# Within-chunk recurrence by halves at six levels instead of by quarters at three

## The chip, the cores and the metric

The kernel runs on one core of one Trainium2 chip. The metric is device time in microseconds (us) of one execution, taken on that core; the median of three runs is given. Engines are named as the profile names them: PE (matrix multiply, with PEld for its weight loads), DVE (vector), ACT (scalar), POOL (GpSimd) and SP (which issues most DMAs here).

## The reference

The kernel computes one decoder block on 528 tokens (16 learned meta tokens ahead of 512 real ones) with 1024 channels: an input projection into nine parts, a gated linear recurrence with 8 heads of 128 keys and 128 values, a short convolution beside it, a merge with gates, an output projection, and a gated feed-forward net of width 2816 with another short convolution. The part that matters here is the recurrence, whose reference runs over chunks:

```python
def step(S, inp):
    qb, kb, vb, gb = inp
    G = jnp.cumsum(gb, axis=-2)
    o_inter = jnp.einsum('bhtd,bhdv->bhtv', qb * jnp.exp(G), S)
    diff = G[:, :, :, None, :] - G[:, :, None, :, :]
    decay = jnp.exp(jnp.where(causal, diff, -jnp.inf))
    A = jnp.sum(qb[:, :, :, None, :] * kb[:, :, None, :, :] * decay, axis=-1)
    o = o_inter + jnp.einsum('bhts,bhsv->bhtv', A, vb)
    ...
```

So a head needs a score matrix A: for each token t and each earlier token s of the chunk, the sum over 128 keys of q(t) k(s) times the product of the forget gates f of the tokens from s+1 to t. Results are float32.

## The kernel before

**Layout.** Channels lie on the 128 partitions and tokens along the free dimension, so q, k, f of one head are tiles of 128 partitions by 528 tokens (`Qs`, `Ks`, `Fs`, two of each, used by head parity; `V_t` for the values). The kernel treats the 512 real tokens as `NCH` = 4 chunks of 128.

**The large products.** Every weight matrix is split on ACT (`wh`, a cast) and DVE (`wl`, the remainder) into two float32r parts, and each product takes three PE passes (lines 323 to 325 in `product`, 426 to 428 in `raw3`). Most are computed two at a time by `Pair`, a scheme with seven products of half size, whose sums of weights are made on DVE (lines 308, 309, 313).

**The recurrence of one head** is the generator `recur` (line 479). Each `yield` ends a step. Before the levels: V is transposed and POOL prepares the meta tokens' decays. Then come three levels with m = 1, 4, 16 (line 509), each of which joins blocks of m tokens, four at a time, into blocks of 4m. At each level:

- `qv`, 192 columns per chunk, is filled: q of the second, third and fourth quarter (ACT, line 523), q of the third and fourth quarter times one quarter's whole decay (DVE, line 525), q of the fourth times two (line 527). `T` holds the whole decay of each block of m tokens, `F` at the first level.
- Four PE matmuls, one per chunk, take K's 128 tokens as stationary operand and the 192 columns of `qv` as moving operand (line 530). The output is a PSUM tile `psq` of 1024 columns, which is two banks; there is one such buffer, and every other use of the pool (`quarter`) takes it too.
- Q is multiplied by the decays up to its place in the new block (lines 531 to 533), K by the decays after its place (line 541), and the decays of the new blocks are formed (ACT line 537, DVE lines 538 to 540).
- Three masked copies (line 546) put the wanted entries of the scores into A.

After the levels a last join with m = 64 is made by halves (lines 551 to 568): four matmuls of 64 stationary and 64 moving columns (line 554), Q and K multiplied (lines 561, 562), the decays of the 128-token chunks (line 564). Four more steps transpose K, form the states S, apply them and A (lines 597, 598), normalize, and transpose back. That is nine steps.

**Order of the work.** All engines follow the order in which the program is written; the Tile framework adds the waits. The large products call `tick` after every six matmuls of a half-width product. `beat` holds a counter and a period: at each multiple of the period, `tick` runs one step of the oldest waiting `recur`. Between two calls of `merge` there are 62 ticks for head 0 (whose counter begins at -4), 64 for heads 1 to 6, and 42 for head 7. The period is 6, and 4 for head 7. `merge(j)` first runs whatever steps of the head are left, and then uses its output `oS` (lines 745, 746).

Of the kernel before, what the change touches and what calls it, by code (L numbers as in the profile page):

```python
# [7 lines left out]
F32 = mybir.dt.float32  # L8
F32R = mybir.dt.float32r
I32 = mybir.dt.int32  # L10
AF = mybir.ActivationFunctionType
ALU = mybir.AluOpType
PSUM = bass.MemoryType.PSUM

P = 128
D = 1024
KT = D // P
NMETA = 16
SEQ = 512
L = NMETA + SEQ  # L20
# [5 lines left out]
NF = DFF // P  # L26
EPS = 1e-6
NCH = SEQ // P
QW = 192
WARM = 40  # L30
GROUPS = (6, 6, 6, 4)
G0 = EARLY = GROUPS[0]
# [24 lines left out]
def block_kernel(ctx: ExitStack, tc: tile.TileContext, xT, par, wts, pairs, ident, masks, finw, out):  # L57
    nc = tc.nc
    dve, act, pe = nc.vector, nc.scalar, nc.tensor

    const = ctx.enter_context(tc.tile_pool(name="const", bufs=1))
# [2 lines left out]
    whl = ctx.enter_context(tc.tile_pool(name="whl", bufs=4))  # L64
    scan = ExitStack()
    ppair = scan.enter_context(tc.tile_pool(name="ppair", bufs=1, space=PSUM))
    pqk = scan.enter_context(tc.tile_pool(name="pqk", bufs=1, space=PSUM))
    po_pool = scan.enter_context(tc.tile_pool(name="po", bufs=1, space=PSUM))
    pmisc = scan.enter_context(tc.tile_pool(name="pmisc", bufs=1, space=PSUM))

    def scores():
        return pqk.tile([P, 1024], F32, name="psq", tag="psq")

    def quarter():
        return scores()[:, :512].rearrange("p (c n) -> p c n", c=NCH)

    def home(i, dtype=F32, n=528, name="t"):
        return big.tile([P, 528], dtype, name=f"{name}{i}", tag=f"b{i}")[:, :n]
# [1 line left out]
    def pbank(i):  # L80
        return ppair.tile([P, 512], F32, name="pr", tag=f"pr{i}", bufs=1 + (i == 0))
# [48 lines left out]
    beat = [0, 5]  # L130
# [84 lines left out]
    par_t = const.tile([P, NPAR], F32, name="par_t")  # L215
    xt = [home(k, name="xt") for k in range(KT)]
    id_t = const.tile([P, P], F32, name="id_t")
    mk_t = const.tile([P, 3, QW], I32, name="mk_t")
    heads = [fetch(4) for _ in range(2)]

    def load_x(k):
# [190 lines left out]
    rstd = p1.tile([P, L], F32, name="rstd")  # L412
# [38 lines left out]
    with tc.tile_pool(name="rp0", bufs=1) as rp:  # L451
        acc = rp.tile([P, L], F32, name="acc")
        firsts = [(split_unit(raw, 4), [pbank(i) for i in q]) for (raw, _), q in zip(heads, ((1, 2), (0, 0)))]
        for k in range(KT):
            if k % 2 == 0:
                firsts[0][0][2][k // 2]()
            split_scaled(uh[k], ul[k], xt[k], pr("attn", k))
            if k % 2 == 0:
                firsts[1][0][2][k // 2]()
            for (h, lo, _), banks in firsts:  # L460
                for o, at in zip(banks, HALF):
                    raw3(o[:, :HL], h[:, k, :], lo[:, k, :], uh[k][:, at], ul[k][:, at], k == 0, k == KT - 1)
            if k == 5:
                h3rd, l3rd, parts = split_unit(third[0])
                parts[0]()
        for k in range(KT):
            add_square(acc, xt[k], rp, L, k)
        for (_, banks), dst in zip(firsts, (Fs[0], Qs[0])):
            for o, at in zip(banks, HALF):
                act.copy(dst[:, at], o[:, :HL])  # L470
        ahead = [load_unit()]
        both = scores()
        spread_rstd(rstd, acc, lambda i: both[:, 512 * i:512 * i + 512], rp, L)
        raw_unit((h3rd, l3rd), lambda o, at: act.copy(V_t[:, at], o))
    p2 = ph.enter_context(tc.tile_pool(name="ph2", bufs=2))

    M1 = NMETA + 1

    def recur(j, oS):
        b = j % 2  # L480
        K, V, F, Q, A = Ks[b], V_t, Fs[b], Qs[b][:, T0:], As[b]
# [23 lines left out]
        nc.gpsimd.tensor_copy(K0[:, 16:17], K[:, 16:17])  # L505
        T = F[:, M1:]
        Qm = Q[:, NMETA - T0:]
        Km_ = K[:, M1:]
        for lev, m in enumerate((1, 4, 16)):
            nb = P // (4 * m)  # L510
            qv = p2.tile([P, NCH, QW], F32, name="qv", tag="qv")
            q4 = Qm.rearrange("p (c b x) -> p c b x", c=NCH, x=4 * m)
            k4 = Km_.rearrange("p (b s m) -> p b s m", s=4, m=m)
            t4 = T.rearrange("p (c b s) -> p c b s", c=NCH, s=4)
            tf = T.rearrange("p (b s) -> p b s", s=4)
            v1 = qv[:, :, :96].rearrange("p c (b x) -> p c b x", x=3 * m)
            v2 = qv[:, :, 96:160].rearrange("p c (b x) -> p c b x", x=2 * m)
            v3 = qv[:, :, 160:].rearrange("p c (b x) -> p c b x", x=m)

            def tb(i):  # L520
                return t4[:, :, :, i:i + 1].to_broadcast([P, NCH, nb, m])

            act.copy(v1, q4[:, :, :, m:])
            for i in range(2):
                dve.tensor_tensor(v2[:, :, :, i * m:(i + 1) * m], q4[:, :, :, (2 + i) * m:(3 + i) * m],
                                  tb(1 + i), op=ALU.mult)
            dve.tensor_tensor(v3, v2[:, :, :, m:], tb(1), op=ALU.mult)
            ps = scores().rearrange("p (c n) -> p c n", c=NCH)
            for c in range(NCH):
                pe.matmul(ps[:, c, :QW], K[:, M1 + c * P:M1 + (c + 1) * P], qv[:, c, :], start=True, stop=True)  # L530
            dve.tensor_tensor(q4[:, :, :, m:2 * m], q4[:, :, :, m:2 * m], tb(0), op=ALU.mult)
            dve.tensor_tensor(q4[:, :, :, 2 * m:3 * m], v2[:, :, :, :m], tb(0), op=ALU.mult)
            dve.tensor_tensor(q4[:, :, :, 3 * m:], v3, tb(0), op=ALU.mult)
            n4 = SEQ // (4 * m)
            tk = p2.tile([P, n4, 3], F32, name=f"TK{lev}", tag=f"TK{lev}")
            tp = p2.tile([P, n4], F32, name=f"T{lev}", tag=f"T{lev}")
            act.copy(tk[:, :, 2], tf[:, :, 3])
            dve.tensor_tensor(tk[:, :, 1], tf[:, :, 2], tf[:, :, 3], op=ALU.mult)
            dve.tensor_tensor(tk[:, :, 0], tf[:, :, 1], tk[:, :, 1], op=ALU.mult)
            dve.tensor_tensor(tp, tf[:, :, 0], tk[:, :, 0], op=ALU.mult)  # L540
            dve.tensor_tensor(k4[:, :, :3, :], k4[:, :, :3, :], tk.unsqueeze(3).to_broadcast([P, n4, 3, m]),
                              op=ALU.mult)
            a4 = A.rearrange("p c (b x) -> p c b x", x=4 * m)
            for r, lo_, hi_ in ((3, 0, 96), (2, 96, 160), (1, 160, QW)):
                mk = mk_t[:, lev, lo_:hi_].rearrange("p (b x) -> p b x", x=r * m)
                dve.copy_predicated(a4[:, :, :, (4 - r) * m:],  # L546
                                    mk.unsqueeze(1).to_broadcast([P, NCH, nb, r * m]),
                                    ps[:, :, lo_:hi_].rearrange("p c (b x) -> p c b x", x=r * m))
            T = tp
            yield  # L550
        ps = quarter()
        for c in range(NCH):
# [10 lines left out]
        T = p2.tile([P, NCH], F32, name="T128", tag="T128")  # L563
# [44 lines left out]
        ps = quarter()  # L608
# [25 lines left out]
    lo_, hi_ = HALF  # L634
# [150 lines left out]
    s = ring()  # L785
# [23 lines left out]
    for q, sink in enumerate((times(cx0), x_sink, b0_sink, gb0_sink)):  # L809
        unit = ahead.pop()  # L810
        ahead.append(load_unit())
        some(1)
        raw_unit(unit, sink)
        some(1)
        if q == 0:
            beat[:] = [-4, 6]
            begin(0)

    def forget(j):
# [21 lines left out]
    for q, (kind, arg) in enumerate(items):  # L841
        if kind == "m":
            if cur:
                cur.last()
                cur = None
            merge(arg)
            if arg + 1 < KT:
                beat[:] = [0, 6 if arg + 2 < KT else 4]
                begin(arg + 1)
        elif kind == "p":  # L850
            w = pair_weights()
            nxt = Pair(w, arg(), HL, lambda: None)
            if cur:
                cur.last()
            cur = nxt
            cur.middle()
        else:
            unit = ahead.pop() if ahead else load_unit()
            sink = arg() if arg.__name__ == "<lambda>" and arg.__code__.co_argcount == 1 else arg
            half_unit(unit, 0, sink)  # L860
            if cur:
                cur.last()
                cur = None
            some(99)
            half_unit(unit, 1, sink)
# [50 lines left out]
    with tc.tile_pool(name="rp1", bufs=1) as rp:  # L916
        acc = fp2.tile([P, LT], F32, name="acc", tag="fa")
        for k in range(KT):
            ps = mtile(mh, ml, LATE)
# [6 lines left out]
        ps = new_ps()  # L926
# [67 lines left out]
    n = 0  # L994
# [57 lines left out]
    tp = ctx.enter_context(tc.tile_pool(name="tp", bufs=1, side="right"))  # L1052
# [4 lines left out]
    for c in range(NCH):  # L1057
        ps = new_ps()
# [20 lines left out]
def _masks():  # L1079
    import numpy as np  # L1080

    s = np.arange(P)[:, None]
    mk = np.zeros((P, 3, QW), np.int32)
    for lev, m in enumerate((1, 4, 16)):
        at = 0
        for r in (3, 2, 1):
            b, x = np.divmod(np.arange(32 * r), r * m)
            sub = 4 - r + x // m
            mk[:, lev, at:at + 32 * r] = (s // (4 * m) == b) & (s // m % 4 == sub - (4 - r))
            at += 32 * r  # L1090
    return mk


# [50 lines left out]
```

## Time and profile before

| what | value |
|---|---|
| median of 3 runs | 899.25 us (899.13 to 899.52) |
| the profiled execution's own time | 899.76 us |
| its span, first to last instruction | 897.8 us |
| PE busy | 879.7 us, 98% of the span |
| PEld busy | 834.7 us, 93% |
| DVE busy | 735.3 us, 82% |
| ACT busy | 513.4 us, 57% |
| mean granted PE clock | 0.997 of full speed |

The heads' recurrences run from about 37 to 482 us of the span, threaded between the large products. Busy times of PE are those of pipelined instructions, which overlap: an instruction's recorded duration is longer than the distance to the next one, and the distance is what counts for throughput. DVE, ACT and PE each run in their own queue, and a wait in one holds up all that is behind it there.

### The profile page before, as it was taken

What the parts mean: (1) busy time and instruction counts of PE and PEld (TensorE: products, weight loads), DVE (VectorE), ACT (ScalarE), POOL (GpSimd) and SP (SyncE); (2) the same over time, 40 slices, a digit from 0 to 9 for tenths busy, and PEclk for the clock granted to TensorE, in tenths of its full rate; (3) what the DMA queues carried; (4) which work ended last, traced back from release to release, by engine and by line L of the source; (5) the groups of instructions that cost most, each with busy time, mean ns of one, the idle gap of its engine ahead of it and who ended that gap; (6) DMA issues with size and microseconds to landing.
All of it is one profiled execution on the core that took longest, in us unless ns stands there. A gap on an engine that the chain in (4) does not pass through costs nothing.

```text
span 897.8 us, 16494 instructions
## 1 busy us (share of the span) xinstructions
PE 879.7 (98%) x6528; PEld 834.7 (93%) x6528; DVE 735.3 (82%) x1320; ACT 513.4 (57%) x946; POOL 37.1 (4%) x100
## 2 busy tenths in 40 slices
PE   9999999999999999999999999999999999999996
PEld 8998999999999999999999999989999999999984
DVE  7899998989979899899777558985778787777665
ACT  8746657566675575765756346554454545545434
POOL 0211030100101002010000000000000000000000
PEclk9999999999999999999999999999999999999998
DMA  7216344333433443343416321453353443534302
GB/s 257 96 42 203 108 142 134 103 120 116 138 104 118 131 123 118 96 141 101 136 27 199 93 89 60 154 159 117 95 169 113 148 135 114 169 95 125 110 24 93
DMA packets 38813, 108.05 MB, mean 120 GB/s; under 512 B 4305, under 2 KB 5585, under 8 KB 38737
## 3 DMA queue, kind: packets, MB, share of 16 engines
q1 hardware_dynamic: 38448, 106.49, 37.6%
q8 instruction: 51, 0.84, 0.4%
q10 hardware_dynamic: 288, 0.52, 0.2%
q14 instruction: 26, 0.20, 0.1%
HBM read 104.90 MB, written 2.10 MB: 119 GB/s over the span
## 4 chain that ended last, share of the span: by engine, by line
PE 81%; DVE 12%; ACT 3%; issue 2%; DMA 1%; SPq 0%; DVEq 0%; ACTq 0%
PE pr L323 15%; PE pr L325 14%; PE pr L324 14%; PE psm L1009 5%; PE psm L1011 4%; PE psm L1010 4%; PE psm L122 4%; PE psm L120 4%; PE psm L119 4%; PE psq L530 2%; DVE wl L299 2%; PE pr L428 2%; PE pr L426 2%; PE pr L427 2%; DVE A L546 1%
## 5 line engine op out<-in xcount | busy, mean ns | idle before, releaser
L323 PE MATMUL pr<-cm,wh 128*128 128x264 f32 x784 | 227.8, 292 | 1.2 <-DVE za L632 0.7
L324 PE MATMUL pr<-cm,wh 128*128 128x264 f32 x784 | 224.4, 287 | 0.0
L325 PE MATMUL pr<-cm,wl 128*128 128x264 f32 x784 | 223.5, 286 | 0.0
L323 PEld LDWEIGHTS pr<-cm,wh 128*128 128x128 f32 x784 | 147.3, 188 | 4.0 <-issue 1.6
L325 PEld LDWEIGHTS pr<-cm,wl 128*128 128x128 f32 x784 | 147.7, 189 | 0.2
L324 PEld LDWEIGHTS pr<-cm,wh 128*128 128x128 f32 x784 | 147.5, 188 | 0.0
L298 ACT CAST wh<-wt 128x1024 fp32r<-128x1024 f32 x88 | 92.6, 1053 | 84.2 <-PE pr L324 44.3
L299 DVE TENSOR_TENSOR wl<-wt,wh 128x1024 fp32r<-128x1024 f32 x88 | 106.9, 1216 | 27.5 <-ACT wh L298 27.5
L100 DVE TENSOR_TENSOR wl<-wr,wh 128x1024 fp32r<-128x1024 f32 (+1 forms) x64 | 71.8, 1126 | 39.1 <-ACT wh L99 37.9
L99 ACT CAST wh<-wr 128x1024 fp32r<-128x1024 f32 (+1 forms) x64 | 61.6, 967 | 67.1 <-PE psm L120 30.2
L331 ACT COPY c<-pr 128x264 f32<-128x264 f32 (+1 forms) x132 | 49.5, 375 | 41.0 <-PE pr L325 36.4
L323 PE MATMUL pr<-cf,wh 128*128 128x258 f32 x256 | 72.5, 283 | 0.0
L324 PE MATMUL pr<-cf,wh 128*128 128x258 f32 x256 | 72.1, 282 | 0.0
L325 PE MATMUL pr<-cf,wl 128*128 128x258 f32 x256 | 71.9, 281 | 0.0
L299 DVE TENSOR_TENSOR wl<-wr,wh 128x1024 fp32r<-128x1024 f32 x44 | 53.8, 1222 | 13.1 <-ACT wh L298 13.0
L298 ACT CAST wh<-wr 128x1024 fp32r<-128x1024 f32 x44 | 46.1, 1048 | 20.6 <-PE pr L324 19.4
L323 PE MATMUL pr<-cb,wh 128*128 128x258 f32 x192 | 54.7, 285 | 0.3 <-ACT xr L970 0.3
L308 DVE TENSOR_TENSOR wt<-wt 128x1024 f32<-128x1024 f32 x44 | 53.7, 1220 | 1.4 <-DMA wt<-in_pairs 1.1
L324 PE MATMUL pr<-cb,wh 128*128 128x258 f32 x192 | 54.7, 285 | 0.0
L325 PE MATMUL pr<-cb,wl 128*128 128x258 f32 x192 | 54.4, 283 | 0.0
L324 PEld LDWEIGHTS pr<-cf,wh 128*128 128x128 f32 x256 | 48.6, 190 | 0.8
L323 PEld LDWEIGHTS pr<-cf,wh 128*128 128x128 f32 x256 | 48.1, 188 | 0.7
(291 smaller groups left out, 2282.7 us busy)
## 6 DMA issues: line engine op xcount, KB each, us to landing
wr<-in_wts SPq DMA_DIRECT2D x56, 512.0 KB, 3.7
wr<-in_pairs SPq DMA_DIRECT2D x44, 512.0 KB, 4.1
wt<-in_pairs SPq DMA_DIRECT2D x44, 512.0 KB, 4.0
wt<-in_pairs SPq DMA_DIRECT2D x88, 256.0 KB, 4.7
xt<-in_xT SPq DMA_DIRECT2D x8, 264.0 KB, 4.8
xr<-in_xT SPq DMA_DIRECT2D x8, 264.0 KB, 3.5
out<-xr SPq DMA_DIRECT2D x8, 256.0 KB, 2.2
wr<-in_wts SPq DMA_DIRECT2D x8, 128.0 KB, 4.5
```

Of the source, the lines that this page charges most:

```text
L99: act.copy(h[:, i:i + n, :], raw[:, i:i + n, :])
L100: dve.tensor_tensor(lo[:, i:i + n, :], raw[:, i:i + n, :], h[:, i:i + n, :].bitcast(F32), op=ALU.subtract)
L119: pe.matmul(o, wh, rh[:, a:b], start=first, stop=False)
L120: pe.matmul(o, wh, rl[:, a:b], start=False, stop=False)
L298: act.copy(h, src)
L299: dve.tensor_tensor(lo, src, h.bitcast(F32), op=ALU.subtract)
L308: dve.tensor_tensor(t[:, 1:3, :], t[:, 1:3, :], t[:, 3:, :].to_broadcast([P, 2, 512]), op=ALU.add)
L323: pe.matmul(ps, h[:, j], ch, start=start and j == 0, stop=False, skip_group_check=True)
L324: pe.matmul(ps, h[:, j], cl, start=False, stop=False, skip_group_check=True)
L325: pe.matmul(ps, lo[:, j], ch, start=False, stop=j == 3, skip_group_check=True)
L331: act.copy(c, r)
L1009: pe.matmul(o, gh, wh, start=first, stop=False)
```

## The change

The three levels by quarters become six levels by halves, with m = 1, 2, 4, 8, 16, 32 (`LEVELS`). A level joins blocks of m tokens, two at a time. The only scores it needs are those of each second half's q against the first half's k, 64 columns per chunk, and these columns are read where they lie in Q, with a stride of 2m, so that `qv` and its ACT copy and DVE multiplies are gone. Q's second halves are then multiplied by the first half's decay, K's first halves by the second half's, the decays of neighbours are multiplied together, and one masked copy of 64 columns per chunk takes the scores into A. The last join with m = 64 and all that follows it are as before.

The PSUM pool `pqk` now has two buffers of one bank each instead of one of two banks. The masks become six of 64 columns instead of three of 192. A head has twelve steps instead of nine, and the periods go from 6 to 5, and from 4 to 3 for head 7.

```diff
-QW = 192
+LEVELS = (1, 2, 4, 8, 16, 32)
...
-    pqk = scan.enter_context(tc.tile_pool(name="pqk", bufs=1, space=PSUM))
+    pqk = scan.enter_context(tc.tile_pool(name="pqk", bufs=2, space=PSUM))
...
-    def scores():
-        return pqk.tile([P, 1024], F32, name="psq", tag="psq")
-
     def quarter():
-        return scores()[:, :512].rearrange("p (c n) -> p c n", c=NCH)
+        return pqk.tile([P, NCH, P], F32, name="psq", tag="psq")
...
-    mk_t = const.tile([P, 3, QW], I32, name="mk_t")
+    mk_t = const.tile([P, len(LEVELS), 64], I32, name="mk_t")
...
-        both = scores()
-        spread_rstd(rstd, acc, lambda i: both[:, 512 * i:512 * i + 512], rp, L)
+        banks = [pqk.tile([P, 512], F32, name="psq", tag="psq") for _ in range(2)]
+        spread_rstd(rstd, acc, lambda i: banks[i], rp, L)
...
-        for lev, m in enumerate((1, 4, 16)):
-            nb = P // (4 * m)
-            qv = p2.tile([P, NCH, QW], F32, name="qv", tag="qv")
...
-            act.copy(v1, q4[:, :, :, m:])
-            for i in range(2):
-                dve.tensor_tensor(v2[:, :, :, i * m:(i + 1) * m], q4[:, :, :, (2 + i) * m:(3 + i) * m],
-                                  tb(1 + i), op=ALU.mult)
-            dve.tensor_tensor(v3, v2[:, :, :, m:], tb(1), op=ALU.mult)
-            ps = scores().rearrange("p (c n) -> p c n", c=NCH)
+        for lev, m in enumerate(LEVELS):
+            nb = P // (2 * m)
+            n2 = SEQ // (2 * m)
+            q2 = Qm.rearrange("p (n h m) -> p n h m", h=2, m=m)
+            k2 = Km_.rearrange("p (n h m) -> p n h m", h=2, m=m)
+            t2 = T.rearrange("p (n h) -> p n h", h=2)
+            ps = quarter()
             for c in range(NCH):
-                pe.matmul(ps[:, c, :QW], K[:, M1 + c * P:M1 + (c + 1) * P], qv[:, c, :], start=True, stop=True)
-            dve.tensor_tensor(q4[:, :, :, m:2 * m], q4[:, :, :, m:2 * m], tb(0), op=ALU.mult)
-            dve.tensor_tensor(q4[:, :, :, 2 * m:3 * m], v2[:, :, :, :m], tb(0), op=ALU.mult)
-            dve.tensor_tensor(q4[:, :, :, 3 * m:], v3, tb(0), op=ALU.mult)
...
-            act.copy(tk[:, :, 2], tf[:, :, 3])
-            dve.tensor_tensor(tk[:, :, 1], tf[:, :, 2], tf[:, :, 3], op=ALU.mult)
-            dve.tensor_tensor(tk[:, :, 0], tf[:, :, 1], tk[:, :, 1], op=ALU.mult)
-            dve.tensor_tensor(tp, tf[:, :, 0], tk[:, :, 0], op=ALU.mult)
-            dve.tensor_tensor(k4[:, :, :3, :], k4[:, :, :3, :], tk.unsqueeze(3).to_broadcast([P, n4, 3, m]),
-                              op=ALU.mult)
...
-            for r, lo_, hi_ in ((3, 0, 96), (2, 96, 160), (1, 160, QW)):
-                mk = mk_t[:, lev, lo_:hi_].rearrange("p (b x) -> p b x", x=r * m)
-                dve.copy_predicated(a4[:, :, :, (4 - r) * m:],
...
-            T = tp
+                pe.matmul(ps[:, c, :64].rearrange("p (b m) -> p b m", m=m), K[:, M1 + c * P:M1 + (c + 1) * P],
+                          q2[:, c * nb:(c + 1) * nb, 1, :], start=True, stop=True)
+            dve.tensor_tensor(q2[:, :, 1, :], q2[:, :, 1, :], t2[:, :, 0:1].to_broadcast([P, n2, m]), op=ALU.mult)
+            dve.tensor_tensor(k2[:, :, 0, :], k2[:, :, 0, :], t2[:, :, 1:2].to_broadcast([P, n2, m]), op=ALU.mult)
+            Tn = p2.tile([P, n2], F32, name=f"T{lev}", tag=f"T{lev}", bufs=1)
+            dve.tensor_tensor(Tn, t2[:, :, 0], t2[:, :, 1], op=ALU.mult)
+            T = Tn
+            dve.copy_predicated(A.rearrange("p c (b h m) -> p c b h m", h=2, m=m)[:, :, :, 1, :],
+                                mk_t[:, lev, :].rearrange("p (b m) -> p b m", m=m).unsqueeze(1)
+                                .to_broadcast([P, NCH, nb, m]),
+                                ps[:, :, :64].rearrange("p c (b m) -> p c b m", m=m))
             yield
...
-            beat[:] = [-4, 6]
+            beat[:] = [-4, 5]
...
-                beat[:] = [0, 6 if arg + 2 < KT else 4]
+                beat[:] = [0, 5 if arg + 2 < KT else 3]
...
-    mk = np.zeros((P, 3, QW), np.int32)
...
+    mk = np.zeros((P, len(LEVELS), 64), np.int32)
+    for lev, m in enumerate(LEVELS):
+        mk[:, lev] = (s // (2 * m) == np.arange(64) // m) & (s // m % 2 == 0)
     return mk
```

More of the change, by code (lines that the diff above doesn't have):

```diff
@@ L508, in recur @@
         Km_ = K[:, M1:]
-        for lev, m in enumerate((1, 4, 16)):
-            nb = P // (4 * m)
-            qv = p2.tile([P, NCH, QW], F32, name="qv", tag="qv")
[L512 to L523, printed above, removed]
-            for i in range(2):
-                dve.tensor_tensor(v2[:, :, :, i * m:(i + 1) * m], q4[:, :, :, (2 + i) * m:(3 + i) * m],
-                                  tb(1 + i), op=ALU.mult)
-            dve.tensor_tensor(v3, v2[:, :, :, m:], tb(1), op=ALU.mult)
-            ps = scores().rearrange("p (c n) -> p c n", c=NCH)
-            for c in range(NCH):
-                pe.matmul(ps[:, c, :QW], K[:, M1 + c * P:M1 + (c + 1) * P], qv[:, c, :], start=True, stop=True)
-            dve.tensor_tensor(q4[:, :, :, m:2 * m], q4[:, :, :, m:2 * m], tb(0), op=ALU.mult)
-            dve.tensor_tensor(q4[:, :, :, 2 * m:3 * m], v2[:, :, :, :m], tb(0), op=ALU.mult)
-            dve.tensor_tensor(q4[:, :, :, 3 * m:], v3, tb(0), op=ALU.mult)
[L534 to L538, printed above, removed]
-            dve.tensor_tensor(tk[:, :, 0], tf[:, :, 1], tk[:, :, 1], op=ALU.mult)
-            dve.tensor_tensor(tp, tf[:, :, 0], tk[:, :, 0], op=ALU.mult)
-            dve.tensor_tensor(k4[:, :, :3, :], k4[:, :, :3, :], tk.unsqueeze(3).to_broadcast([P, n4, 3, m]),
-                              op=ALU.mult)
-            a4 = A.rearrange("p c (b x) -> p c b x", x=4 * m)
-            for r, lo_, hi_ in ((3, 0, 96), (2, 96, 160), (1, 160, QW)):
-                mk = mk_t[:, lev, lo_:hi_].rearrange("p (b x) -> p b x", x=r * m)
-                dve.copy_predicated(a4[:, :, :, (4 - r) * m:],
-                                    mk.unsqueeze(1).to_broadcast([P, NCH, nb, r * m]),
-                                    ps[:, :, lo_:hi_].rearrange("p c (b x) -> p c b x", x=r * m))
-            T = tp
@@ L1082, in _masks @@
     s = np.arange(P)[:, None]
-    mk = np.zeros((P, 3, QW), np.int32)
[L1084 to L1090, printed above, removed]
+    mk = np.zeros((P, len(LEVELS), 64), np.int32)
+    for lev, m in enumerate(LEVELS):
+        mk[:, lev] = (s // (2 * m) == np.arange(64) // m) & (s // m % 2 == 0)
     return mk
```

## The prediction, made before the changed kernel was run

> **What bounds the kernel now.** I read the page first, then what PE waits for, then PE's timeline around the matmuls that the change touches, then the rows of the DVE and ACT instructions that go. The page's busy times, and its chain of waits by engine:
>
> ```profile
> PE 879.7 (98%) x6528; PEld 834.7 (93%) x6528; DVE 735.3 (82%) x1320; ACT 513.4 (57%) x946; POOL 37.1 (4%) x100
> PE 81%; DVE 12%; ACT 3%; issue 2%; DMA 1%; SPq 0%; DVEq 0%; ACTq 0%
> ```
>
> PE is busy 98% of the time and holds 81% of the chain. The chain's 12% on DVE looks like a second bound, but it is not 12% that could be won: where PE waits 0.5 us for DVE, the chain changes to DVE and follows it back through everything that it did back to back. What a faster DVE can win is what PE really waits. Those waits of PE that lie in the recurrences' stretch are these (total us, times, longest):
>
> ```profile
> PE psq L554 <- DVE A L546: 1.3, 2, 1.0
> PE pr L428 <- DVE wl L100: 1.0, 2, 0.5
> PE psq L579 <- ACT Km L576: 0.7, 1, 0.7
> PE pr L323 <- DVE za L632: 0.7, 1, 0.7
> PE psq L530 <- DVE qv L525: 0.6, 1, 0.6
> PE psm L119 <- DVE z L726: 0.5, 1, 0.5
> PE pm L612 <- DVE om L606: 0.5, 1, 0.5
> PE pr L323 <- ACT c L331: 0.5, 1, 0.5
> PE po L597 <- ACT S L583: 0.4, 1, 0.4
> PE psq L530 <- DVE qv L527: 0.2, 1, 0.2
> ```
>
> They sum to 6.4 us in 12 waits. A wait costs a little more than its row says, since PE counts as busy until its pipeline has drained. The longest one, in the timeline (start, length, instruction, count, idle time before):
>
> ```profile
> 407.69 0.28 PE L325 MATMUL pr<-cm,wl 128*128 128x264 f32 x1
> 409.01 0.65 PE L554 MATMUL psq<-Q,K 128*64 128x64 f32 x8 [1.04 <-DVE A L546]
> ```
>
> Without the wait L554 would have started one product distance (0.12 us, below) after 407.69; it started 1.20 us later than that, of which the row shows 1.04. So a wait costs 0.16 us beyond its row, and the 12 cost 6.4 + 12 x 0.16 = 8.3 us. That is all that lies within reach of a lighter DVE and ACT; the rest of this stretch is PE going from matmul to matmul. So the question is how much PE time the change adds or takes.
>
> **PE: the price of one pass.** A float32 matmul is issued as two passes, each with its own load of the stationary operand: line 530 runs 12 times for each of 8 heads, and the trace has 192 of it (lengths of single passes, which overlap: minimum, median, maximum in ns).
>
> ```profile
> L530 PE MATMUL psq<-qv,K x192: 323/326/402, 48.1 to 457.2; 128*128 128x192 f32 x192
> L197 PE MATMUL psq<-onesD,acc x10: 242/250/250, 21.2 to 22.2; 128*128 128x1 f32 x10
> L554 PE MATMUL psq<-Q,K x64: 222/222/271, 67.9 to 462.3; 128*64 128x64 f32 x64
> ```
>
> The distance from one pass to the next comes out of the timeline's merged rows: the length of the row less that of one pass, over the count less one.
>
> ```profile
> 396.35 0.28 PE L325 MATMUL pr<-cm,wl 128*128 128x264 f32 x1
> 396.47 1.46 PE L530 MATMUL psq<-qv,K 128*128 128x192 f32 x8
> ...
> 397.89 0.28 PE L427 MATMUL pr<-cm,wh 128*128 128x264 f32 x1
> 398.01 0.28 PE L428 MATMUL pr<-cm,wl 128*128 128x264 f32 x1
> ...
> 21.23 1.25 PE L197 MATMUL psq<-onesD,acc 128*128 128x1 f32 x10 [0.25 <-DVE acc L176]
> ...
> 425.16 0.28 PE L325 MATMUL pr<-cm,wl 128*128 128x264 f32 x1
> 425.28 0.38 PE L597 MATMUL po<-S,Q 128*128 128x128 f32 x2
> ...
> 427.18 0.28 PE L324 MATMUL pr<-cm,wh 128*128 128x264 f32 x1
> ```
>
> - 192 moving columns, 128 stationary: (1.46 - 0.326) / 7 = 162 ns. The whole insert agrees: from 396.35 to 397.89 are 1.54 us, less two product distances of 0.12 (397.89 to 398.01) is 1.30, or 8 x 162 ns. Such an insert costs nothing at its edges.
> - 128 moving, 128 stationary: from 425.16 to 427.18, less 0.24, are 1.78 us for the 16 passes of lines 597 and 598: 111 ns.
> - 1 moving, 128 stationary: (1.25 - 0.250) / 9 = 111 ns.
> - 64 moving, 64 stationary (line 554, row above): (0.65 - 0.222) / 7 = 61 ns.
>
> From 192 to 128 moving columns the distance falls, and from 128 to 1 it no longer does. So 111 ns is a floor that the 128 stationary float32 columns set, with the moving columns passing beside their load; line 554 goes lower with half as many. **The new matmuls have 64 moving columns but still 128 stationary ones** (a whole chunk of K), so I give each pass 111 ns, as in the rows on either side, 1 and 128.
>
> The Trainium skill has two rules that part here. "TensorE: Matmul & The Clock Gate", section "Back-to-back issue gap", lists about 60 cycles (25 ns) for a matmul of up to 64 columns; by that the 384 new passes are an estimated 9.6 us against 31.1 now, 21.5 us gained. Its section "LDWEIGHTS (loading the stationary operand)" has the load scale with the stationary columns alone, 107 ns for 128 of them; by that they are an estimated 41.1 us, 10.0 lost. The trace sides with the second: 111 ns at one moving column, 61 at half the stationary ones.
>
> Per head before: 24 passes x 162 = 3.89 us. After: 6 levels x 4 chunks x 2 = 48 passes x 111 = 5.33 us. **PE gets 1.44 us more work a head, 11.5 us over 8 heads**, and it is the bound all through this stretch: + 11.5.
>
> **DVE and ACT: what goes.** What the levels hold now, and the nearest rows to what they will hold (the row with the sum is line 546 in one stretch per head):
>
> ```profile
> L525 DVE TENSOR_TENSOR qv<-Q,T x32: 261/282/490, 55.5 to 451.2; 128x128 f32<-128x128 f32 x32
> L525 DVE TENSOR_TENSOR qv<-Q,F x16: 378/397/416, 46.3 to 400.6; 128x128 f32<-128x128 f32 x16
> L538 DVE TENSOR_TENSOR TK<-T x16: 164/190/210, 57.7 to 414.1; 128x32 f32<-128x32 f32 x8, 128x8 f32<-128x8 f32 x8
> L538 DVE TENSOR_TENSOR TK<-F x8: 389/438/471, 48.4 to 402.3; 128x128 f32<-128x128 f32 x8
> L541 DVE TENSOR_TENSOR K<-K,TK x24: 545/552/608, 50.0 to 458.2; 128x384 f32<-128x384 f32 x24
> sum 246.00, DVE 38.95; mean DVE 4.87
> L546 DVE COPY_PREDICATED A<-mk_t,psq 128x256 f32<-128x256 int32 x24 | 12.9, 538 | 0.0
> L561 DVE TENSOR_TENSOR Q<-Q,T x8: 407/414/425, 68.8 to 462.5; 128x256 f32<-128x256 f32 x8
> L523 ACT COPY qv<-Q x24: 497/514/518, 37.3 to 447.7; 128x384 f32<-128x384 f32 x24
> ACT qv L523 <- PE psq L530: 12.9, 15, 1.0
> ACT TK L537 <- DVE T L540: 10.5, 12, 1.4
> ```
>
> Now, per head: 18 multiplies of 128 elements (lines 525, 527, 531 to 533), 12 at 0.28 and the first level's 6 at 0.40, are 5.8 us; 9 of lines 538 to 540, 6 at 0.19 and 3 at about 0.4, are 2.3; line 541 is 1.7; the masked copies 4.9. That is 14.7 us. After: six times Q and K (0.41 each) and one masked copy of 256 elements (0.54) are 8.2 us, and six products of decays, from 256 elements down to 8, at 0.19 to 0.44 are about 1.5: 9.7 us. DVE loses 5 us a head; ACT loses its copies (0.51 us three times a head) and the 23 us in which its queue stood behind them (the last two rows).
>
> None of this is on PE's path except through the 8.3 us. Of the waits, L530's two and L554's two (2.1 us, 2.7 with the drain) belong to what the change takes away: L530 waits for `qv`, made in its own step, while the new matmuls read Q and K as the step before left them; and L554 waits for the masked copies to give back the one `psq`, of which there are now two. These count as won. Four rows (L428, L323 after `za`, L579, L597: 2.8 us in 5 waits, 3.6 with the drain) come from queues that are late, and the trace has the first head as the stretch without slack on DVE:
>
> ```profile
> 30.00:97.00 67.00, 63.99 (x501) 61.19 (x500) 65.49 (x139) 41.44 (x84) 10.95 (x20) 1.00 0.36 116
> ```
>
> (The length of the stretch, then PE, PEld and DVE busy: DVE 65.5 of 67 us.) I count half of the 3.6 as won, since the splits and sums in that queue stay. The last three (L119, L612, L323 after `c`) stand near the ends of heads, and I count none. Together 4.5 us won, between 0 (waits only move) and 8.3.
>
> **What is added beside PE's passes.** The multiplies of Q and K must wait until the level's matmuls have read them, and the masked copy until they have written. Behind them on DVE stand the `wl` splits and the sums of the pairs, for which PE's later products wait. This happens six times a head instead of three. Two levels are 5 ticks apart, 30 products of 0.12 us and the level's own 0.9: 4.5 us, for 0.8 us of DVE work (Q and K) that the next level needs. For head 7 it is 3 ticks, 2.2 + 0.9 = 3.1 us. Head 0 reaches 55 as its last multiple of 5, so `merge` runs its twelfth step; DVE's line 745 then waits for the transposes and their copy, some 1 us at most, while PE goes on with the next pair's first product, which needs none of it. No row shows what an insert pays whose operands DVE has only just finished; the bounds are nothing (L530's edges) and one drain of 0.16 for each of 24 inserts more, 3.8. I take 1.0 for all of this, nearer the row of the same kind. The masks' transfer shrinks by a third and nothing early waits for it, and `spread_rstd` uses two buffers where it used two halves of one: nothing.
>
> **Sum.** Against the profiled execution's own 899.76 us: + 11.5 - 4.5 + 1.0 = + 8.0, so 907.8. That execution is 0.5 above the median of the runs shown; for the median, 899.25 + 8.0 = **907.2 us**.
>
> **Rivals.**
>
> 1. *The load does not set the distance* (this ends on the other side). If the load of K's columns hides, and the 111 ns at one moving column has another cause, the new passes go at line 554's 61 ns: 384 x 61 = 23.4 us against 31.1, 7.7 gained, and with the 3.5 (4.5 less 1.0) 899.25 - 7.7 - 3.5 = 888.0. It decides from the distance at which 384 passes take 31.1 + 3.5: below 90 ns the change gains. For it speaks that no row has 64 moving on 128 stationary; against it, that the rows on either side both say 111. The issue-gap rule above is its strongest form. Chance 0.10, half of it between.
> 2. *All waits go.* 899.25 + 11.5 - 8.3 = 902.5. For it, DVE's 65.5 of 67 us in the first stretch; against it, that the last three waits stand far from the levels. Still slower, since 11.5 exceeds all that PE waits. Chance 0.08.
> 3. *Head 7's closer steps wait.* DVE does runs of three long operations there:
>
> ```profile
> 445.27 1.22 DVE L299 TENSOR_TENSOR wl<-wt,wh 128x1024 fp32r<-128x1024 f32 x1
> 446.41 1.22 DVE L308 TENSOR_TENSOR wt<-wt 128x1024 f32<-128x1024 f32 x1
> 447.54 1.22 DVE L299 TENSOR_TENSOR wl<-wt,wh 128x1024 fp32r<-128x1024 f32 x1
> ```
>
>    If one such run (3.6 us) falls between two levels, the next comes 3.6 + 0.8 - 3.1 = 1.3 us late; once for each of head 7's three pairs, 3.9 us in place of the 1.0: 910.1. It decides from 2.3 us of other work between two levels. Against it, PE waited for `qv` at only two of the 24 levels before, though `qv` is made in the level's own step on the same queue. Chance 0.14.
> 4. *Strided reads.* At m = 1 Q is read with a stride of two elements. DVE's rows (397 against 282 ns at the first level) show that strides can cost. PE has room: at 61 ns the columns may pass 1.8 times slower inside 111. At three times, 183 ns, the 128 passes of two levels would cost 72 ns more each, 9.2 us: 916.4. Chance 0.03.
>
> The forecast itself has 0.65.
>
> **Numbers.** The range runs from the case in which all waits go, 902.5, to 912.0, which holds rival 3 and the edges at their most (907.2 - 1.0 + 3.8 = 910.0) with 2 us for waits that aren't won. It leaves out rival 1 and rival 4. A measurement of this kernel tells about 0.2%, 1.8 us, from no change. Slower by more than that is everything but rival 1, 0.90; rival 1 gives 0.05 faster and 0.05 within.
>
> **What would show it.** Right: 384 passes in the levels' line, in merged rows of 8 that last about 0.25 + 7 x 0.111 = 1.03 us; few waits of PE on the levels' tiles; DVE some 40 us less busy; 1.4 us more PE work a head. Wrong: such rows near 0.68 us, waits of PE for Q, K or `psq` in head 7, or a time under 901.

## The result, and the profile after

| | before | changed kernel |
|---|---|---|
| median | 899.19 us (898.96 to 899.52, 4 runs) | 910.18 us (909.49 to 911.37, 4 runs) |
| ratio | | 1.0123, 95% interval 1.0106 to 1.0141 |
| profiled execution: own time, span | 899.76, 897.8 us | 911.37, 909.6 us |

The changed kernel is slower, 11.0 us by the medians and 11.6 by the two profiled executions. The page's busy times and chain of waits after:

```profile
PE 892.8 (98%) x6720; PEld 848.4 (93%) x6720; DVE 715.4 (79%) x1200; ACT 498.9 (55%) x898; POOL 31.4 (3%) x100
PE 94%; DVE 2%; ACT 1%; DMA 1%; issue 0%; SPq 0%; ACTq 0%; DVEq 0%
```

PE is busy 13.1 us longer and holds 94% of the chain, where it held 81%; DVE's 12% of the chain are down to 2%, and that bought no time. One insert of a level in PE's timeline, with products before and after it:

```profile
227.41 0.28 PE L322 MATMUL pr<-cm,wl 128*128 128x264 f32 x1
227.53 1.00 PE L514 MATMUL psq<-Q,K 128*128 128x64 f32 x8
228.34 0.37 PE L320 MATMUL pr<-cm,wh 128*128 128x264 f32 x1
228.55 0.28 PE L321 MATMUL pr<-cm,wh 128*128 128x264 f32 x1
```

From 227.41 to 228.55 are 1.14 us; less two product distances of 0.12 the insert takes 0.90, or 112 ns for each of its 8 passes. The 33 other inserts that stand whole between two products, with no wait beside them, take 0.89 or 0.90, but for one of 1.06. An insert took 1.30 before, but there were half as many. The very first level of a head, whose columns are read with a stride of two elements, takes the same (222.85 to 223.99 in head 2):

```profile
222.85 0.29 PE L322 MATMUL pr<-cm,wl 128*128 128x264 f32 x1
222.98 1.00 PE L514 MATMUL psq<-Q,K 128*128 128x64 f32 x8
223.79 0.37 PE L423 MATMUL pr<-cm,wh 128*128 128x264 f32 x1
223.99 0.28 PE L424 MATMUL pr<-cm,wh 128*128 128x264 f32 x1
```

What PE waits for in the recurrences' stretch (total us, times, longest), and one wait of DVE:

```profile
PE pr L425 <- DVE wl L97: 3.0, 1, 3.0
PE pr L320 <- ACT c L328: 1.3, 1, 1.3
PE psm L116 <- DVE z L701: 0.5, 1, 0.5
PE pm L587 <- DVE om L581: 0.2, 1, 0.2
...
DVE Q L516 <- PE psq L514: 17.7, 32, 1.3
```

Together they are 5.0 us in 4 waits, where the kernel before had 6.4 in 12. The waits on the levels' tiles are gone: no row of PE names line 514 or 529 (the old 530 and 554). DVE's new wait at each level, 17.7 us in all, reaches PE nowhere as a row of its own. But there is one wait of 3.0 us, longer than any before, and a second of 1.3. The first, on PE and on DVE's queue:

```profile
66.66 0.59 PE L425 MATMUL pr<-cm,wl 128*128 128x264 f32 x1 [2.98 <-DVE wl L97]
67.04 0.42 PE L423 MATMUL pr<-cm,wh 128*128 128x264 f32 x1
67.26 0.42 PE L424 MATMUL pr<-cm,wh 128*128 128x264 f32 x1
...
72.32 0.32 PE L425 MATMUL pr<-cm,wl 128*128 128x264 f32 x1
72.48 0.29 PE L423 MATMUL pr<-cm,wh 128*128 128x264 f32 x1
72.61 0.29 PE L424 MATMUL pr<-cm,wh 128*128 128x264 f32 x1
```

```profile
59.16 0.43 DVE L516 TENSOR_TENSOR Q<-Q,T 128x256 f32<-128x256 f32 x1 [0.43 <-PE psq L514]
59.50 0.70 DVE L365 TENSOR_TENSOR cm<-ct,cm 128x528 fp32r<-128x528 f32 x1
60.12 0.70 DVE L391 TENSOR_TENSOR ct<-hn 128x528 f32<-128x528 f32 x1
60.74 0.70 DVE L379 TENSOR_TENSOR ct<-hn 128x528 f32<-128x528 f32 x1
61.36 0.42 DVE L517 TENSOR_TENSOR K<-K,T 128x256 f32<-128x256 f32 x1
...
65.35 1.26 DVE L97 TENSOR_TENSOR wl<-wr,wh 128x1024 fp32r<-128x1024 f32 x1
```

Two things are to be seen. The weight split that PE waits for (line 97) stands in DVE's queue behind a run of sums for later products (lines 365 to 391). And the queue isn't in the written order: lines 516, 517, 519 and 521 are written one after another, but three operations of other work stand between 516 and 517. So my sentence that all engines follow the order in which the program is written was wrong: the queues get an order of their own, and a change in one place can move instructions in another (wide_move, below, changes only the levels' matmuls and their masked copy, and there this split starts at 57.61 instead of 65.35). What sets the order was not looked into.

The second thing is what the wait did to PE's clock. Products came 0.22 us apart from 67.04 on, and 0.12 apart again from 72.5. The windows' row for that stretch (length, DVE busy, granted clock, then DMA):

```profile
65.00:75.00 10.00, 7.54 (x15) 0.66 0.69 239
```

In the kernel before, the granted clock is 1.00 throughout the same stretch. From 66.66 to 72.32 some 26 products took 0.10 us more each, about 2.6 us. So this one wait cost some 3.1 us of standing still and 2.6 of half speed. In windows of 1 us the clock falls at about 65.6, 1.9 us into the idle time, and is back at 72.4, after 6.8 us at half. The same wait of 3.0 us stands in two of the runs below: in half_load the clock fell 1.2 us into it and stayed at half for 6.8 us, in after_phase at its end, and for 3.4 us. So the cost in clock is not the same each time, and the 2.6 us are those of this execution, the longest of the changed kernel's four. "TensorE: Matmul & The Clock Gate" in the Trainium skill has PE return to half rate after an idle window of about 3.4 us that runs freely (section "What's actually happening"); the trace agrees on the half rate, and 3.4 and 6.8 us at half would be one and two such windows, but here 3.0 us idle were enough, and the clock had fallen before they were over.

### The profile page after: what moved, and what is told of

Its sections match the earlier page's. It is cut to its first block, busy times and chain, and to the rows that moved or that the text cites. A ratio compares the mean times of both kernels' runs of the same rounds, so it can differ in the third digit from the quotient of the medians.

```text
span 909.6 us, 16754 instructions
## 1 busy us (share of the span) xinstructions
PE 892.8 (98%) x6720; PEld 848.4 (93%) x6720; DVE 715.4 (79%) x1200; ACT 498.9 (55%) x898; POOL 31.4 (3%) x100
## 4 chain that ended last, share of the span: by engine, by line
PE 94%; DVE 2%; ACT 1%; DMA 1%; issue 0%; SPq 0%; ACTq 0%; DVEq 0%
PE pr L320 17%; PE pr L321 16%; PE pr L322 16%; PE psm L984 4%; PE psm L986 4%; PE psq L514 4%; PE psm L985 4%; PE psm L119 4%; PE psm L116 4%; PE psm L117 4%; PE pr L425 3%; PE pr L423 3%; PE pr L424 3%; PE psq L556 1%; PE po L573 1%; PE po L572 1%
## 5 line engine op out<-in xcount | busy, mean ns | idle before, releaser
L320 PE MATMUL pr<-cf,wh 128*128 128x258 f32 x256 | 72.5, 283 | 0.0
```

What stands on the lines that cost most here:

```text
L320: pe.matmul(ps, h[:, j], ch, start=start and j == 0, stop=False, skip_group_check=True)
```

## The experiments

Theory L was that the load of the stationary operand sets the price of a pass, so that twice the loads are the loss. Its rival M was that the price goes by moving columns, and the loss came from the steps. (A price that each pass has whatever it loads is a third reading; only half_load tells it from L.) On the 1.3 and 3.0 us waits, theory W put them on the closer steps, and V on the order of the queues.

**Twice the loads alone (cut_two).** The kernel before, with each matmul in two:

```diff
-pe.matmul(ps[:, c, :QW], K[:, M1 + c * P:M1 + (c + 1) * P], qv[:, c, :], start=True, stop=True)
+for u, w in ((0, 128), (128, QW)):
+    pe.matmul(ps[:, c, u:w], K[:, M1 + c * P:M1 + (c + 1) * P], qv[:, c, u:w], start=True, stop=True)
```

> The kernel before, by quarters, with each matmul of 192 moving columns cut into one of 128 and one of 64 on the same stationary chunk of K: as many loads as the change makes (48 passes a head instead of 24), the same columns, the same DVE and ACT work, steps and periods. Theory L (the load of 128 stationary columns sets the price of a pass, 111 ns): 384 passes x 111 ns = 42.6 us against 31.1, so 899.2 + 11.5 = 910.7 us, within 2 us for waits that move. Rival M (the price goes by moving columns, and the loss came from the steps by halves): 2304 columns a head as before, so 899.2 us.

Measured: 909.88 us against 899.37, ratio 1.0105 (1.0086 to 1.0125). One level of it:

```profile
281.46 0.28 PE L428 MATMUL pr<-cm,wl 128*128 128x264 f32 x1
281.58 1.89 PE L531 MATMUL psq<-qv,K 128*128 128x128 f32 x16
283.28 0.37 PE L426 MATMUL pr<-cm,wh 128*128 128x264 f32 x1
283.49 0.28 PE L427 MATMUL pr<-cm,wh 128*128 128x264 f32 x1
```

From 281.46 to 283.49, less 0.24, are 1.79 us for 16 passes, 112 ns each, whether they move 128 columns or 64. Over 24 inserts, 1.79 for 1.30 is 11.8 us. Twice the loads, with no column more and nothing else in the program changed, cost 10.5 us, about what the whole change cost; some of PE's waits moved as well (4.4 us in this stretch for 6.4, with a new one of 2.1 us for ACT's line 606). M falls.

**Twice the columns alone (wide_move).** The changed kernel, with all of a chunk's Q moving:

```diff
-pe.matmul(ps[:, c, :64].rearrange("p (b m) -> p b m", m=m), K[:, M1 + c * P:M1 + (c + 1) * P],
-          q2[:, c * nb:(c + 1) * nb, 1, :], start=True, stop=True)
+pe.matmul(ps[:, c, :], K[:, M1 + c * P:M1 + (c + 1) * P], Qm[:, c * P:(c + 1) * P], start=True, stop=True)
...
-                    ps[:, :, :64].rearrange("p c (b m) -> p c b m", m=m))
+                    ps.rearrange("p c (b h m) -> p c b h m", h=2, m=m)[:, :, :, 1, :])
```

> The changed kernel, with all 128 columns of a chunk of Q as moving operand, read without stride, instead of the 64 that are needed; the masked copy takes the same entries. Theory L: the columns pass beside the load, so 112 ns a pass as before, 910.2 us within 1.5. Rival M: at 0.8 ns a column (the difference of the rows for 192 and 128) 64 columns more are 51 ns a pass, 19.6 us, 929.8 us. If the stride in Q had cost something, this would be faster than 910.2.

Measured: 905.81 us, ratio to the kernel before 1.0062 (1.0043 to 1.0080), so 4.4 us *faster* than the changed kernel and not 19.6 slower. One level:

```profile
222.47 0.28 PE L322 MATMUL pr<-cm,wl 128*128 128x264 f32 x1
222.59 1.05 PE L514 MATMUL psq<-Q,K 128*128 128x128 f32 x8
223.40 0.37 PE L320 MATMUL pr<-cm,wh 128*128 128x264 f32 x1
223.61 0.28 PE L321 MATMUL pr<-cm,wh 128*128 128x264 f32 x1
```

From 222.47 to 223.61, less 0.24: 0.90 us, what 64 columns took. Twice the columns are free beside the load. The 4.4 us can therefore not come from the stride, which my expectation had offered as the reading of a faster time; the passes' price is the same. They fit head 0's 5.7, less two waits that are new here (0.8 us for line 580, 0.4 for line 517): this kernel has no wait of PE for line 97 at all, since its queues came out in another order, and its clock is 1.00 there. The same split in DVE's queue:

```profile
57.61 1.22 DVE L97 TENSOR_TENSOR wl<-wr,wh 128x1024 fp32r<-128x1024 f32 x1
```

That was the first sign for V.

**Half the load (half_load).** The changed kernel, with 64 stationary columns:

```diff
-pe.matmul(ps[:, c, :64].rearrange("p (b m) -> p b m", m=m), K[:, M1 + c * P:M1 + (c + 1) * P],
+pe.matmul(ps[:64, c, :64].rearrange("p (b m) -> p b m", m=m), K[:, M1 + c * P:M1 + c * P + 64],
           q2[:, c * nb:(c + 1) * nb, 1, :], start=True, stop=True)
```

(The masked copy takes 64 partitions accordingly.)

> The changed kernel, with only the first 64 tokens of each chunk as stationary operand of a level's matmul, so that scores of the other 64 against later tokens are left out; as many matmuls, moving columns and DVE instructions. Theory L: a pass costs what line 554 showed for 64 stationary columns, 61 ns, so 384 x (112 - 61) = 19.6 us less than the changed kernel, 910.2 - 19.6 = 890.6 us, up to 3 more where DVE can no longer keep up. Rival M (moving columns or a fixed cost of each pass): no change, 910.2 us.

Measured: 905.64 us, ratio 1.0059 (1.0036 to 1.0082): 4.5 us less than the changed kernel, where L had said 19.6 and M nothing. The trace shows why L was short:

```profile
224.70 0.28 PE L322 MATMUL pr<-cm,wl 128*128 128x264 f32 x1
224.91 0.68 PE L514 MATMUL psq<-Q,K 128*64 128x64 f32 x8
225.52 0.39 PE L320 MATMUL pr<-cm,wh 128*128 128x264 f32 x1
225.75 0.28 PE L321 MATMUL pr<-cm,wh 128*128 128x264 f32 x1
```

Within the insert the passes do come 65 ns apart, (0.68 - 0.222) / 7, as line 554 had shown. But from 224.70 to 225.75, less 0.24, are 0.81 us, and 8 x 65 ns are 0.52: an insert of narrower stationary operands pays 0.29 us at its edges. Against 0.90 that is 0.09 saved for each of 48 inserts, 4.3 us, which is what was measured; 38 inserts of this run lie between 0.80 and 0.84, and head 0's wait and half clock are in it as in the changed kernel. So L stands for the distance between passes, and a price that each pass has whatever it loads falls. My expectation failed by edges that I had not counted. They could have been seen in the kernel before, at line 554:

```profile
461.61 0.28 PE L324 MATMUL pr<-cm,wh 128*128 128x264 f32 x1
461.82 0.68 PE L554 MATMUL psq<-Q,K 128*64 128x64 f32 x8
462.43 0.39 PE L325 MATMUL pr<-cm,wl 128*128 128x264 f32 x1
462.66 0.28 PE L323 MATMUL pr<-cm,wh 128*128 128x264 f32 x1
```

From 461.61 to 462.66, less 0.24, are 0.81 us here too: 101 ns a pass with the edges, where within the row they are 61 to 65 ns apart. What makes them was not tried.

**The periods alone (periods).** The kernel before, with 5 and 3 for 6 and 4:

```diff
-beat[:] = [-4, 6]
+beat[:] = [-4, 5]
...
-beat[:] = [0, 6 if arg + 2 < KT else 4]
+beat[:] = [0, 5 if arg + 2 < KT else 3]
```

> The kernel before with the periods of the change, 5 and 3 instead of 6 and 4, and nothing else. The changed kernel has two new long waits of PE, 3.0 us in head 0 and 1.3 us at the end of head 7. Theory W (the closer steps make them): they come here too, and with L530's own waits the time is 902 to 904 us. Rival V (they come from the order in which DVE and ACT stand in their queues, which is planned anew for each kernel): no such pair here, 899.2 us within 1.5.

Measured: 898.47 us, ratio 0.9986 (0.9976 to 0.9997). Closer steps cost the kernel by quarters nothing, and its longest wait in the levels' stretch is 0.6 us:

```profile
PE psq L530 <- DVE A L546: 0.7, 2, 0.6
```

W falls for these levels; on the levels by halves the periods were not changed alone.

**Head 0's split, earlier (after_early).** If the order of DVE's queue is the cause, moving one split up is the cure:

```diff
 unit = ahead.pop() if ahead else load_unit()
+if q < 2:
+    ahead.append(load_unit())
```

> The changed kernel, with the second and third weight units of head 0's row of single units loaded and split one unit earlier in the program, nothing else. In the changed kernel's DVE queue that split (line 97, at 65.35 us) stands behind ten operations of the combinations and PE waits 3.0 us for it. Theory V (the planned order of DVE's queue in head 0 ate the gain that I had counted): the wait goes, 910.2 - 3 to 4.5 = 905.7 to 907.2 us. Rival D (DVE has too much to do there in any order): the wait moves to a later unit and the time stays within 1 us of 910.2.

Measured: 907.10 us (906.77 to 907.60), ratio 1.0089 (1.0075 to 1.0102), 3.1 us less than the changed kernel. In the written order, too, the split had stood behind those sums, and the edit puts it ahead of them. It now starts at 56.94, and the longest waits of PE in the recurrences' stretch are:

```profile
PE pr L320 <- ACT c L328: 1.3, 1, 1.3
...
PE pm L587 <- DVE om L581: 0.9, 1, 0.9
PE pr L322 <- DVE wl L296: 0.6, 1, 0.6
```

The 3.0 us wait and the half clock behind it are gone. Two waits of 0.9 (0.2 before) and 0.6 came in their place, so that 4.2 or so of the 5.7 us of wait and clock should come back. The two profiled executions are 4.5 apart (911.37 and 906.91), the medians 3.1; the changed kernel's profiled execution is its longest, and of its others no trace is kept. V holds for head 0, as far as the place in the queue goes: what the edit moved is the split, and the wait went with it.

**Head 7, one tick earlier (after_phase).** For the other wait, 1.3 us for ACT's line 328:

```diff
-beat[:] = [0, 5 if arg + 2 < KT else 3]
+beat[:] = [0, 5] if arg + 2 < KT else [1, 3]
```

> The changed kernel, with head 7's counter beginning at 1 instead of 0, so that each of its steps comes one tick earlier. In the changed kernel PE waits 1.3 us at 489 us for ACT line 328, which stands behind the square root of head 7's eleventh step. If the place of that step beside the pair's products makes the wait, it shrinks to the 0.5 us that it had before: 909.2 us; if the wait comes from ACT's work there in any order, 910.2 us as it was.

Measured: 910.14 us (909.11 to 911.62). The wait is what the first theory said:

```profile
PE pr L320 <- ACT c L328: 0.5, 1, 0.5
```

What stands ahead of line 328 in the changed kernel is shown by ACT's queue:

```profile
489.06 1.28 ACT L183 ACT_TABLE_LOAD   x1
490.36 0.21 ACT L183 ACTIVATE ryo<-rvo 128x5 f32<-128x5 f32 x1
490.47 0.36 ACT L328 COPY c<-pr 128x264 f32<-128x264 f32 x1
```

It is less the square root itself, 0.21 us, than the load of its table, 1.28 us. In after_phase that load comes at 485.56, behind a copy of line 328 and 2.5 us ahead of the next. The time did not follow within what its runs can show: 0.04 us less, where 1.0 was expected, with runs spread over 2.5 us. That the tick's place made the wait is shown by the trace; that it is worth 1 us is not.

**The kernel by quarters, with both (periods_early).** The two edits above that had not hurt, on the kernel before:

> The kernel before, with the periods 5 and 3 and with the second and third weight units of head 0 split one unit earlier. If what is left of PE's waits in head 0 (L428 for line 100, 0.9 us with two drains of 0.16) goes: 898.5 - 1.2 = 897.3 us; if DVE is full there in any order: 898.5 us. Either way under the 899.2 of the kernel before.

Measured: 896.55 us (895.75 to 897.77, 8 runs), ratio 0.9971 (0.9961 to 0.9981), the fastest of all here, 2.6 us under the kernel before and 13.6 under the changed one. The longest that is left in the levels' stretch:

```profile
PE psq L530 <- DVE A L546: 1.0, 2, 0.6
PE pr L323 <- ACT c L331: 0.6, 1, 0.6
PE pr L428 <- DVE wl L100: 0.5, 1, 0.5
```

It gained 1.9 over the periods alone (1.7 when each is held against the kernel before that was measured beside it), where I had said 1.2, though L428's wait only went from 0.9 to 0.5; which of the small waits made the rest, I can't tell from these rows.

## Why the prediction was right, and where not

I had said 907.2 us, 902.5 to 912.0, slower; it is 910.18.

- *The bound.* Right. PE's share of the chain rose from 81% to 94%. The chain's share on DVE fell from 12% to 2% and nothing was won by it: as the prediction argued, it had been the path's detour over short waits.
- *The price of a pass, 111 ns, + 11.5 us.* Right: 112 in the trace, for 64 columns as for 128. 48 inserts of 0.90 us for 24 of 1.30 are + 12.0, and cut_two, with the loads alone, cost 10.5 in its medians.
- *DVE and ACT.* Line by line right (Q and K at 0.42, a head's levels near 9.7 us), but DVE's busy time fell by 20 us and not by 40. The recorded lengths of the levels' lines did fall by 41 us (119 to 78). Such a sum overstates what goes: DVE's operations overlap, and in the rows above an operation of 0.70 us is followed by the next after 0.62.
- *Waits won, - 4.5.* This is the step that failed. Its first part, 2.7 us for the waits on `qv` and on the one `psq`, came true: both are gone. Its second, "half of the 3.6" of the queues that are late in the first head, did not. I had read those waits as DVE having too much to do, and given it less; what counted was where an instruction stands in its queue, and the order came out anew. In its place came one wait of 3.0 us, and a half clock that no part of the prediction had, some 5.7 us together, where the five waits had been 3.6. In all, the four waits left in this stretch are 5.0 us, 5.6 with the drains and 8.2 with the clock, against 8.3 in the kernel before: nothing was won, which is the lower bound that I had named (waits only move). With the passes' 12.0 that gives the 11.6 by which the two profiled executions differ, within half a microsecond. after_early shows the cause: with the split moved up, the wait and the half clock go. That its 907.1 is the forecast to 0.1 us is partly luck, since the waits left there (1.3, 0.9, 0.6, 0.5) are not the ones that I had counted as left.
- *What is added, + 1.0.* The edges of the inserts were nothing, as at L530. Head 0's twelfth step made no wait that I could find. The wait at the end of head 7 grew from 0.5 to 1.3; after_phase shows that it hangs on the tick at which the square root's table load falls, not on the number of steps.
- *Rivals.* The first is out (cut_two, wide_move). Its price was misread besides: line 554's 61 ns leave out the edges, and with them its 8 passes take 0.81 us, so 48 such inserts would have been 38.9 us against 31.1, 7.8 lost and not 7.7 gained. The second would have needed all waits gone; they did not go. The third named head 7, and PE waits for nothing at the levels there; periods shows the closer steps harmless on the levels by quarters. The fourth is out: the first level's insert takes 0.90 us like the others.

## What to carry to other kernels

Count a small float32 matmul by its stationary load first: with 128 stationary columns anything up to 128 moving columns cost the same 112 ns here, so halving the moving columns and doubling the matmuls is a loss on a bound PE, and widening the moving operand up to there is free. A lighter engine off the path pays only where PE waits for it, and such waits can hang on the order of a queue, which a change elsewhere in the program can alter; look at what stands ahead of the late instruction, and move that instruction, before taking work away. A wait of 3 us on PE may cost nearly as much again in the clock.

## What I had not expected of the hardware

- One wait of PE of 3.0 us halved its granted clock until 5.7 us after the wait ended (0.66 over a stretch of 10 us; products 0.22 instead of 0.12 us apart), about 2.6 us more. In two other runs with the same wait it was 5.1 and 3.5 us. The clock fell 1.9 us into the idle time, and 1.2 and 3.0 in the two others.
- An insert of matmuls with 64 stationary columns between products with 128 pays 0.29 us at its edges, while one with 128 pays none; so the narrower load, 65 instead of 112 ns a pass, saved 0.09 us of 0.90 on 8 passes.
- Moving columns read with a stride of two float32 elements cost PE nothing beside a load of 112 ns.
